# Probabilities split into two float16 parts in SBUF and turned by transposing DMAs, with four PSUM banks for scores

## The chip, the core and the metric

The kernel runs on one core of a Trainium2 chip. The metric is device time in microseconds (us) of one launch. The engines of the core are TensorE (PE; its weight loads are listed apart as PEld), VectorE (DVE), ScalarE (ACT), GpSimd (POOL) and SyncE (SP), which here issues all DMAs from one queue, in order. PE writes to PSUM, which has eight banks of 512 float32 per partition; everything else lies in SBUF.

## What is computed

One layer of a hybrid encoder for 1,024 positions of width 1,024: a layer norm, one input projection into sixteen column groups, four mixers, gates, one output projection, and a second layer norm. Three of the mixers are attentions with four heads of 64, and they are where the change lies:

```python
# B: each chunk of 64 positions sees itself and the 8 chunks before it
s = einsum(q, k) * 64 ** -0.5 + rel_bias;  p = softmax(s);  o = einsum(p, v)
# C: an indexer scores all keys, the best 256 are kept
score = einsum(relu(iq . ik) * 64 ** -0.5, iw * 8 ** -0.5)
_, idx = top_k(score, 256);  p = softmax(q . k[idx] * 64 ** -0.5 + t5_bias);  o = p . v[idx]
# M: 256 memory tokens
p = softmax(q . km * 64 ** -0.5);  o = p . vm
# together (A is a gated MLP over blocks of 128 positions)
mixed = concat(ya * silu(a_g), yb * silu(b_g), yc * silu(c_g), ym * silu(m_g))
out = layer_norm(2 ** 0.25 * h + mixed @ w_out + b_out)
```

## The kernel before

Rows are worked on in eight blocks of 128 (`rb`), heads in pairs (`pair`, `odd`). Float32 operands of projections and scores are split into a high and a low float32r part, and a product is three matmuls (high x high, high x low, low x high). A projection (`project`) is 24 matmuls of 128x512 into one bank; its weight block comes by DMA (`raw`), is rounded by ACT and gets its low part from POOL (`wblk`, line 203).

An attention is a list of items, one per row block and head pair: 16 for memory (M), 16 for band attention (B), 16 for sparse attention (C). Each item has four sorts of parts. `scores` makes the score matmuls into banks `qk`, adds the bias with a running maximum (DVE) and takes the exponential (ACT) into a float32 row tile `sc`, up to 1,024 wide. `turn` transposes up to four 128x128 blocks of `sc` on PE into a bank `pt`; `spread` rounds that to float16 (`ph`, on ACT) and takes the rest (`pl`, on DVE). `values` multiplies both by the values, kept as three bfloat16 parts (`pv_mm`), and normalises. `close` turns the output once on PE, multiplies it by the gate and stores it to `mix_dram`. There are 64, 120 and 144 blocks to turn in M, B and C, 328 in all, in 112 groups.

`parts_of` writes the order: with the scores of an item come the turns and all but the last values of the item before it, the last values of the one before that, and the close of a third. `weave` puts steps of a projection between these parts; a `Filler` step may stand on PE no earlier than the part that lies `LAG` (for output projections `LAG_O`) parts back. `OUT_PER` is how many steps of the output projection follow a part in the last attentions, `OUT_FROM` where that begins. The search for the 256 best scores runs beside it on DVE and ACT (`jka`, `jk`). The final order on each engine is made by the scheduler, which takes these priorities and its own simulated times.

`BANKS` shares out PSUM: 2 banks for projections (`pp`), 2 for scores (`qk`), 3 for transposes (`pt`), 1 for values (`pv`).

Of the kernel before, what the change touches and what calls it, by code (L numbers as in the profile page):

```python
# [11 lines left out]
F32 = mybir.dt.float32  # L12
# [32 lines left out]
LAG_O = 14  # L45
# [9 lines left out]
LAG, LAG_S = 22, 6  # L55
# [20 lines left out]
def tile_trunk(ctx, tc, x, mem, ln_in_g, ln_in_b, w_in, b_in, a_ln_g, a_ln_b, a_ws, a_bs,  # L76
# [112 lines left out]
    def wblock(w, c0, m=P):  # L189
# [4 lines left out]
        if m < P:  # L194
            both = gp.tile([P, 2, 2, KT // 2, m], F32R, tag="planes", bufs=1, name="wnar")
        for q in range(2):
            t = E.tile([P, 2, 4, P], F32R, tag="w", bufs=WB, name="wblk") if m == P else both[:, q]
# [96 lines left out]
    def x_parts(half, xts):  # L294

        high, rest = hT[half]
        for k in range(KT):
            pt = bank(("pt", "qk")[k % 2], "xT")
# [11 lines left out]
    def mem_parts(r, mt):  # L310
        for q in range(2):
            pt = bank("pt")
# [206 lines left out]
    def spread(pt, n):  # L519

        ph = gp.tile([P, 512], F16, tag="ph", bufs=3, name="ph")
        pl = gp.tile([P, 512], F16, tag="pl", bufs=3, name="pl")
# [4 lines left out]
    def pv_mm(pv, j, ph, pl, c, v3, first, last):  # L527
        PE.matmul(pv[:, j * 192:j * 192 + 192], ph[:, c:c + P], v3.rearrange("p t d -> p (t d)"),
                  start=first, stop=False)
        PE.matmul(pv[:, j * 192:j * 192 + 128], pl[:, c:c + P], v3[:, 0:2].rearrange("p t d -> p (t d)"),  # L530
# [18 lines left out]
    gates = {}  # L549

    def gate_of(kt, rb):
        if (kt, rb // 4) not in gates:
            t = gp.tile([P, 512], F32, tag="gate", bufs=2, name="gate")
            SP.dma_start(out=t, in_=gate_dram[kt][rb // 4])
            gates[kt, rb // 4] = t
        c = (rb % 4) * P
        return gates[kt, rb // 4][:, c:c + P]
# [4 lines left out]
    class Item:  # L562
# [3 lines left out]
        def __init__(self, scores, turn, values, close=None):  # L566
            self.scores, self.turn, self.values, self.close = scores, turn, values, close

    def parts_of(items):
# [3 lines left out]
        for t in range(n + 3):  # L573
            now, prev, prev2, prev3 = [items[t - d] if 0 <= t - d < n else None for d in range(4)]
# [56 lines left out]
    def mix_of_m(pair, rb, q):  # L631
# [14 lines left out]

        def turn():
            pt = bank("pt")
            for j in range(4):
                PE.transpose(pt[:, j * P:(j + 1) * P], d["sc"][:, j * P:(j + 1) * P], ident)  # L650
            d["p"] = spread(pt, 512)

        def values():
            ph, pl = d["p"]
            pv = bank("pv")
            for odd in range(2):
                for r in range(2):
                    pv_mm(pv, odd, ph, pl, (2 * odd + r) * P, v3m[pair][:, r, odd], r == 0, r == 1)
            d["o"] = normalized(pv, d["rsum"], 6)

        def close():
            t = small([P, P], "mix")
# [3 lines left out]
        return Item(scores, [turn], [values], close)  # L666

    def mix_of(kt, rb, kb0, st, near, far_of, last):
# [31 lines left out]

        def turn(odd, c):
            sc = d["sc"][odd]
            m = min(4, nk - c)
            pt = bank("pt")
            for j in range(m):
# [610 lines left out]
```

## Time and profile before

| | |
|---|---|
| median of 3 timed runs | 700.78 us (699.7 to 700.86) |
| the profiled execution | 701.02 us, of which the span from first to last instruction is 699.1 |
| PE, DVE, ACT, POOL busy | 660.8, 527.4, 415.7, 259.1 us |
| granted clock of PE, mean | 0.993 |
| DMA | 63.49 MB, all issued by SP |

Busy time is the union of an engine's instructions. Matmuls overlap and their ends are modelled, so the mean duration of a matmul is longer than the slot it takes in the queue; the slot is the distance between starts. A wait is put down to the instruction whose signal came last.

### The profile page before, as it was taken

What the parts mean: (1) busy time and instruction counts of PE and PEld (TensorE: products, weight loads), DVE (VectorE), ACT (ScalarE), POOL (GpSimd) and SP (SyncE); (2) the same over time, 40 slices, a digit from 0 to 9 for tenths busy, and PEclk for the clock granted to TensorE, in tenths of its full rate; (3) what the DMA queues carried; (4) which work ended last, traced back from release to release, by engine and by line L of the source; (5) the groups of instructions that cost most, each with busy time, mean ns of one, the idle gap of its engine ahead of it and who ended that gap; (6) DMA issues with size and microseconds to landing.
All of it is one profiled execution on the core that took longest, in us unless ns stands there. A gap on an engine that the chain in (4) does not pass through costs nothing. (4 is left out here: it accounts for less than half of the span.)

```text
span 699.1 us, 11217 instructions
## 1 busy us (share of the span) xinstructions
PE 660.8 (95%) x3882; PEld 507.6 (73%) x3882; DVE 527.4 (75%) x1376; ACT 415.7 (59%) x865; POOL 259.1 (37%) x254
## 2 busy tenths in 40 slices
PE   4889999999999998989999999999899998999895
PEld 3767877776777776767777777777678676777685
DVE  6684235556868989897787879999965789698735
ACT  4764345554789697967787789465355554344210
POOL 4672212530624554132110221022222536457752
PEclk9999999999999999999999999999999999999998
DMA  9792510311321232222110312122102473134111
GB/s 271 229 340 77 167 31 7 115 46 32 101 82 48 76 107 61 75 84 54 57 39 11 89 33 58 29 65 84 53 5 72 150 253 102 68 118 166 57 61 60
DMA packets 67444, 63.49 MB, mean 91 GB/s; under 512 B 9232, under 2 KB 55612, under 8 KB 67388
## 3 DMA queue, kind: packets, MB, share of 16 engines
q1 hardware_dynamic: 67388, 62.78, 29.4%
q8 instruction: 30, 0.49, 0.3%
q14 instruction: 26, 0.21, 0.1%
HBM read 46.70 MB, written 17.64 MB: 92 GB/s over the span
## 5 line engine op out<-in xcount | busy, mean ns | idle before, releaser
L91 PE MATMUL acc<-hTh,wblk 128*128 128x512 f32 (+1 forms) x960 | 311.1, 395 | 3.2 <-ACT hTh L91 1.3
L91 PEld LDWEIGHTS acc<-hTh,wblk 128*128 128x128 f32 x960 | 176.8, 188 | 48.4 <-issue 10.5
L91 PE MATMUL acc<-hTl,wblk 128*128 128x512 f32 (+1 forms) x480 | 186.5, 389 | 0.0
L203 POOL TENSOR_TENSOR wblk<-raw,wblk 128x512 fp32r<-128x512 f32 x72 | 99.1, 1380 | 191.0 <-ACT wblk L91 186.5
L91 PEld LDWEIGHTS acc<-hTl,wblk 128*128 128x128 f32 x480 | 90.4, 188 | 17.5 <-issue 1.8
L91 ACT ACTIVATE jka<-score,cand 128x768 int8<-128x768 f32 (+2 forms) x93 | 96.6, 1039 | 8.3 <-DVE cand L91 6.1
L91 ACT ACTIVATE ph<-pt 128x512 f16<-128x512 f32 (+3 forms) x112 | 51.4, 476 | 37.7 <-PE pt L91 34.8
L91 DVE TENSOR_TENSOR pl<-pt,ph 128x512 f16<-128x512 f32 (+3 forms) x112 | 59.4, 540 | 12.7 <-ACT ph L91 12.2
L91 ACT ACTIVATE sc<-sc,nb 128x640 f32<-128x640 f32 (+7 forms) x64 | 46.6, 730 | 37.4 <-DVE nb L91 37.2
L91 DVE SCALAR_TENSOR_TENSOR score<-relu,iw,score 128x384 f32<-128x384 f32 (+5 forms) x42 | 45.1, 1078 | 20.0 <-ACT relu L91 17.4
L91 ACT ACTIVATE wblk<-raw 128x512 fp32r<-128x512 f32 x72 | 44.5, 628 | 23.5 <-PE acc L91 13.4
L91 PE MATMUL pt<-ident,sc 128*128 128x128 f32 x328 | 57.2, 280 | 0.0
L91 PE MATMUL acc<-woh,mh 128*128 128x512 f32 (+1 forms) x144 | 55.7, 387 | 0.0
L91 PE MATMUL acc<-wol,mh 128*128 128x512 f32 (+1 forms) x144 | 54.2, 377 | 0.0
L91 PE MATMUL acc<-woh,ml 128*128 128x512 f32 (+1 forms) x144 | 54.0, 377 | 0.0
L91 ACT ACTIVATE relu<-sc 128x384 f32<-128x384 f32 (+2 forms) x80 | 36.3, 530 | 25.9 <-PE sc L91 25.8
L91 PE MATMUL pv<-v,ph 128*128 128x192 bf16 x264 | 47.0, 249 | 3.2 <-ACT ph L91 2.6
L91 PEld LDWEIGHTS <-ph 128*128 128x128 f16 x328 | 32.1, 98 | 18.9 <-issue 9.9
L91 PEld LDWEIGHTS pt<-ident,sc 128*128 128x128 f32 x328 | 38.5, 142 | 7.3 <-issue 1.9
L91 PE MATMUL pv<-v,pl 128*128 128x128 bf16 x264 | 43.7, 222 | 0.1
L91 PEld LDWEIGHTS <-pl 128*128 128x128 f16 x328 | 31.6, 98 | 12.3 <-DVE pl L91 3.5
L91 DVE TENSOR_SCALAR_CACHE_REDUCE jk<-planes,lo 128x384 bf16<-128x384 uint16 (+2 forms) x48 | 35.7, 744 | 1.0
(206 smaller groups left out, 1255.9 us busy)
## 6 DMA issues: line engine op xcount, KB each, us to landing
raw<-in_w_in SPq DMA_DIRECT2D x32, 512.0 KB, 3.9
xt<-in_x SPq DMA_DIRECT2D x8, 512.0 KB, 8.6
h_dram<-xt SPq DMA_DIRECT2D x8, 512.0 KB, 5.8
gate<-t SPq DMA_DIRECT2D x16, 256.0 KB, 2.1
rawo<-in_w_out SPq DMA_DIRECT2D x8, 512.0 KB, 4.7
hr<-h_dram SPq DMA_DIRECT2D x8, 512.0 KB, 6.2
out<-hr SPq DMA_DIRECT2D x7, 512.0 KB, 2.7
gate<-gate SPq DMA_DIRECT2D x13, 256.0 KB, 2.7
```

Of the source, the lines that this page charges most:

```text
L91: ins = op(*a, **k)
L203: G.tensor_sub(t[:, 1], r, f32(t[:, 0]))
```

## The change

The two parts of the probabilities are made in SBUF, before they are turned: ACT rounds `sc` to float16, POOL subtracts (`part`). Both parts are written where there is room, mostly in the second half of the `sc` tile seen as float16 (`row`), or over the scores already used. A transposing DMA, issued by SP, then turns up to eight 128x128 blocks into a tile `pT`, of which there are six (`turn`). An item of 512 keys or fewer takes one such DMA for each head (an M item one for both), one of 640 two, one of 768 and more three: 124 in all. PE's 328 transposes of probabilities and `spread` are gone; the turn of the output in `close` stays on PE.

Scores get four banks, transposes one. `parts_of` has no turns any more: all of an item's values come two items after its scores. The gates are loaded in pieces of 128x128, one per item, in place of 128x512. Weight tiles go from five to four, and the lags and shares of the woven projections change.

```diff
-LAG_O = 14
+LAG_O = 9
...
-LAG, LAG_S = 22, 6
+LAG, LAG_S = 15, 4
...
-C1_ORDER, C1_HELD, HELD_PARTS, HELD_STEPS = "k0 k1 v1 q1 v0 g1", "q0 g0", 5, 16
-OUT_FROM, OUT_PER = 3, 1
-S4, EV, WB, SB, BOOST = 8, 4, 5, 4, 400
-BANKS = {"pp": 2, "qk": 2, "pt": 3, "pv": 1}
+C1_ORDER, C1_HELD, HELD_PARTS, HELD_STEPS = "k0 k1 v1 q1 v0 g1", "q0 g0", 2, 16
+OUT_FROM, OUT_PER = 2, 1.5
+S4, EV, WB, SB, BOOST = 8, 4, 4, 4, 400
+TB = 6
+BANKS = {"pp": 2, "qk": 4, "pt": 1, "pv": 1}
...
-                accs = [bank(("qk", "pt")[odd], "sc") for odd in range(2)]
+                accs = [bank("qk", "sc") for _ in range(2)]
...
-    def spread(pt, n):
...
-        S.activation(ph[:, :n], pt[:, :n], AF.Copy)
-        V.tensor_sub(pl[:, :n], pt[:, :n], ph[:, :n])
-        return ph, pl
...
+    def turned(sc, n):
...
+        row, nb = sc.bitcast(F16), n // P
+
+        def part(a, b, high, rest):
+            S.activation(high, sc[:, a:b], AF.Copy)
+            G.tensor_sub(rest, sc[:, a:b], high)
+
+        def turn(t, a, src):
+            SP.dma_start_transpose(out=t[:, a:a + src.shape[-1] // P, :], in_=src)
+
+        t = gp.tile([P, KT, P], F16, tag="pT", bufs=TB, name="pT")
+        if 4 * n <= 2048:
+            part(0, n, row[:, 2 * n:3 * n], row[:, 3 * n:4 * n])
+            turn(t, 0, row[:, 2 * n:4 * n])
+            return [t[:, j] for j in range(nb)], [t[:, nb + j] for j in range(nb)]
+        u = gp.tile([P, KT, P], F16, tag="pT", bufs=TB, name="pT")
+        if 3 * n <= 2048:
+            high = row[:, 2 * n:3 * n]
+            part(0, n, high, row[:, :n])
+            turn(t, 0, high)
+            turn(u, 0, row[:, :n])
+            return [t[:, j] for j in range(nb)], [u[:, j] for j in range(nb)]
+        if 2 * n + 512 <= 2048:
+            high = row[:, 2 * n:2 * n + 512]
+        else:
+            high = gp.tile([P, 512], F16, tag="high", bufs=2, name="high")
+        part(0, 512, high, row[:, :512])
+        turn(t, 0, high)
+        part(512, n, row[:, 512:n], row[:, 1024:512 + n])
+        turn(u, 0, row[:, :n])
+        turn(t, 4, row[:, 1024:512 + n])
+        return ([(t, u)[j > 3][:, j] for j in range(nb)], [(u, t)[j > 3][:, j] for j in range(nb)])
...
+    def gate_of(kt, rb):
+        t = gp.tile([P, P], F32, tag="gate", bufs=2, name="gate")
+        SP.dma_start(out=t, in_=gate_dram[kt][rb // 4][:, (rb % 4) * P:(rb % 4 + 1) * P])
+        return t
...
             if prev2:
-                parts.append(prev2.values[-1])
-            if prev:
-                parts.append(prev.turn[0])
-            if prev3 and prev3.close:
+                parts.append(prev2.values[0])
+            if prev3:
                 parts.append(prev3.close)
-            if prev:
-                for turn, values in zip(prev.turn[1:], prev.values):
-                    parts += [turn, values]
+            if prev2:
+                parts += prev2.values[1:]
...
                 S.activation(sc[:, :n], sc[:, :n], AF.Exp, bias=nb, accum_out=d["rsum"][:, odd:odd + 1])
-
-        def turn(odd, c):
-            sc = d["sc"][odd]
-            m = min(4, nk - c)
-            pt = bank("pt")
-            for j in range(m):
-                PE.transpose(pt[:, j * P:(j + 1) * P], sc[:, (c + j) * P:(c + j + 1) * P], ident)
-            d["p", odd, c] = spread(pt, m * P)
+                d["p", odd] = turned(sc, n)
```

What this moves on PE, at the end of a band item's values in the second pair (before; `ph` and `pl` are the float16 parts, `o` the output of an earlier item, `acc` a projection):

```order
L91 LDWEIGHTS ph_4368
L91 MATMUL pv_4321<-v3_3150,ph_4368 128x192
L91 LDWEIGHTS pl_4369
L91 MATMUL pv_4321<-v3_3150,pl_4369 128x128
L91 MATMUL pt_4464<-ident_66,o_4278 128x128
L91 MATMUL pt_4471<-ident_66,sc_4229 128x128
L91 MATMUL pt_4492<-ident_66,sc_4230 128x128 x4
L91 MATMUL acc_4612<-hTl1_116,wblk_4286 128x512
```

And the same sort of place after, where the values of the item two back follow the scores (`qk`) of a later one:

```order
L92 MATMUL qk_5172<-kl_3933,qh_3664 128x256
L92 MATMUL qk_5173<-kl_3933,qh_3664 128x256
L92 MATMUL acc_5121<-hTh0_113,wblk_5117 128x512
L92 MATMUL acc_5121<-hTl0_114,wblk_5117 128x512
L92 MATMUL acc_5121<-hTh0_113,wblk_5117 128x512 x2
L92 LDWEIGHTS pT_4966
L92 MATMUL pv_5206<-v3_4195,pT_4966 128x192
L92 LDWEIGHTS pT_4967
L92 MATMUL pv_5206<-v3_4195,pT_4967 128x128
```

The transposes of `sc` no longer stand between values and projections; the weights of the value matmuls are slices of `pT`, which DMAs fill.

SP's queue where memory attention begins, after (before, the weight loads stand there without anything between them; `raw` is a weight block, `mix` the output of an item, `gate` a gate):

```order
L193 DMA raw_2620<-in_w_in 128x8x128
L531 DMA_TRANSPOSE pT_2088<-sc_2085 128x8x128
L193 DMA raw_2628<-in_w_in 128x8x128
L531 DMA_TRANSPOSE pT_2131<-sc_2128 128x8x128
L193 DMA raw_2852<-in_w_in 128x8x128
L531 DMA_TRANSPOSE pT_2157<-sc_2154 128x8x128
L531 DMA_TRANSPOSE pT_2218<-sc_2215 128x8x128
L584 DMA mix0_101<-mix_2272 128x128
L580 DMA gate_2440<-gate6_0_97 128x128
L531 DMA_TRANSPOSE pT_2301<-sc_2298 128x8x128
```

The transposing DMAs stand in the one queue behind loads that wait for buffers and behind stores that wait for earlier items' outputs, and those stand behind them.

## Rows read from the trace of the kernel before

**Rows 1.** The page's head: busy us of each engine, share, instructions.
```profile
span 699.1 us, 11217 instructions
PE 660.8 (95%) x3882; PEld 507.6 (73%) x3882; DVE 527.4 (75%) x1376; ACT 415.7 (59%) x865; POOL 259.1 (37%) x254
```

**Rows 2.** Stretches: busy PE, PEld, DVE, ACT, POOL; clock, DMA share, GB/s.
```profile
204.00:333.00 129.00, 121.94 (x723) 93.77 (x723) 113.89 (x336) 106.17 (x233) 51.70 (x68) 1.00 0.26 74
333.00:483.00 150.00, 149.41 (x891) 111.74 (x891) 129.92 (x446) 109.47 (x233) 26.24 (x21) 1.00 0.18 52
483.00:545.00 62.00, 59.62 (x380) 45.82 (x379) 47.55 (x125) 29.07 (x60) 16.34 (x16) 1.00 0.19 58
545.00:655.00 110.00, 105.33 (x663) 80.09 (x661) 90.81 (x236) 50.94 (x117) 65.66 (x59) 0.98 0.40 131
655.00:699.10 44.10, 36.45 (x201) 31.61 (x200) 22.95 (x39) 4.98 (x10) 19.31 (x20) 0.93 0.16 62
```

**Rows 3.** The chain that ended last, from 655 us: start, us, what.
```profile
662.65 28.81 PE acc L91 x172
...
691.49 0.43 DVE hr L91
...
695.32 0.66 DVEq L1312
```

**Rows 4.** The page's groups of turns and splits: busy us, mean ns, idle.
```profile
L91 ACT ACTIVATE ph<-pt 128x512 f16<-128x512 f32 (+3 forms) x112 | 51.4, 476 | 37.7 <-PE pt L91 34.8
L91 DVE TENSOR_TENSOR pl<-pt,ph 128x512 f16<-128x512 f32 (+3 forms) x112 | 59.4, 540 | 12.7 <-ACT ph L91 12.2
...
L91 PE MATMUL pt<-ident,sc 128*128 128x128 f32 x328 | 57.2, 280 | 0.0
```

**Rows 5.** PE's timeline in the late attentions: start us, us, instruction.
```profile
601.71 0.60 PE L91 MATMUL pt<-ident,sc 128*128 128x128 f32 x4
602.07 0.48 PE L91 MATMUL acc<-woh,mh 128*128 128x512 f32 x1
602.38 0.40 PE L91 MATMUL acc<-wol,mh 128*128 128x512 f32 x1
602.62 0.39 PE L91 MATMUL acc<-woh,ml 128*128 128x512 f32 x1
```

**Rows 6.** Groups by form on ACT and POOL.
```profile
L91 ACT ACTIVATE wblk<-raw 128x512 fp32r<-128x512 f32 x72 | 44.5, 628 | 23.5 <-PE acc L91 13.4 <-DMA raw<-in_w_in 4.7 <-DMA raw<-in_w_mem_kv 3.2
L91 ACT ACTIVATE ph<-pt 128x512 f16<-128x512 f32 x60 | 35.1, 590 | 23.8 <-PE pt L91 23.7
L91 ACT ACTIVATE sc<-sc,nb 128x640 f32<-128x640 f32 x20 | 16.4, 824 | 5.3 <-DVE nb L91 5.3
...
L203 POOL TENSOR_TENSOR wblk<-raw,wblk 128x512 fp32r<-128x512 f32 x72 | 99.1, 1380 | 191.0 <-ACT wblk L91 186.5 <-PE sc L91 1.9 <-PE qk L91 1.8
L1176 POOL TENSOR_TENSOR hr<-hr,bo 128x1024 f32<-128x1024 f32 x7 | 17.7, 2543 | 0.1
```

**Rows 7.** Waits of PEld and SP: who for whom, us in total, times, longest.
```profile
PEld L91 <- ACT ph L91: 5.5, 4, 2.8
PEld L91 <- DVE pl L91: 3.5, 5, 1.8
PEld qk L91 <- DVE mx L91: 2.9, 4, 2.1
PEld acc L91 <- POOL wblk L203: 2.2, 2, 1.1
...
SPq L192 <- POOL wblk L203: 157.7, 28, 25.2
```

**Rows 8.** DMA issues: KB each, median us from issue to landing.
```profile
raw<-in_w_in SPq DMA_DIRECT2D x32, 512.0 KB, 3.9
...
gate<-gate SPq DMA_DIRECT2D x13, 256.0 KB, 2.7
...
bias<-in_b_in SPq DMA_DIRECT2D x1, 13.0 KB, 8.0
```

**Rows 9.** The tile `sc`: ns min/median/max, first and last start us, forms.
```profile
L91 ACT ACTIVATE sc<-sc,nb x64: 386/768/1152, 335.3 to 639.0; 128x640 f32<-128x640 f32 x20, 128x128 f32<-128x128 f32 x8, 128x256 f32<-128x256 f32 x8, 128x384 f32<-128x384 f32 x8
...
L91 ACT ACTIVATE sc<-qk,nb x32: 463/474/491, 204.3 to 326.8; 128x256 f32<-128x256 f32 x32
...
L91 DVE CUSTOM_DVE_ANT_0 sc<-qk,farB x24: 285/552/558, 346.6 to 469.9; 128x384 f32<-128x384 f32 x16, 128x128 f32<-128x128 f32 x4, 128x256 f32<-128x256 f32 x4
L91 DVE CUSTOM_DVE_ANT_0 sc<-qk,nearB,mx x24: 472/480/485, 347.1 to 476.3; 128x256 f32<-128x256 f32 x24
```

More of the change, by code (lines that the diff above doesn't have):

```diff
@@ L194, in wblock @@
         if m < P:
-            both = gp.tile([P, 2, 2, KT // 2, m], F32R, tag="planes", bufs=1, name="wnar")
+            narrow = [gp.tile([P, 2, KT // 2, m], F32R, tag=tag, bufs=1, name="wnar") for tag in ("planes", "score6")]
         for q in range(2):
-            t = E.tile([P, 2, 4, P], F32R, tag="w", bufs=WB, name="wblk") if m == P else both[:, q]
+            t = E.tile([P, 2, 4, P], F32R, tag="w", bufs=WB, name="wblk") if m == P else narrow[q]
             r = raw[:, 4 * q:4 * q + 4, :m]
@@ L297, in x_parts @@
         for k in range(KT):
-            pt = bank(("pt", "qk")[k % 2], "xT")
+            pt = bank("qk", "xT")
             for j in range(4):
@@ L311, in mem_parts @@
         for q in range(2):
-            pt = bank("pt")
+            pt = bank("qk", "mT")
             for j in range(4):
@@ L516, in tile_trunk, with pv_mm @@
                 V.memset(score[rb][0:64, (rb + 1) * P - 64:(rb + 1) * P], LOW)
[L519 to L528 removed]
+    def turned(sc, n):
[27 more added lines that the diff above has]
+        return ([(t, u)[j > 3][:, j] for j in range(nb)], [(u, t)[j > 3][:, j] for j in range(nb)])
+    def pv_mm(pv, j, ph, pl, v3, first, last):
+        PE.matmul(pv[:, j * 192:j * 192 + 192], ph, v3.rearrange("p t d -> p (t d)"),
                   start=first, stop=False)
[L530 removed]
+        PE.matmul(pv[:, j * 192:j * 192 + 128], pl, v3[:, 0:2].rearrange("p t d -> p (t d)"),
                   start=False, stop=last)
@@ L562, in tile_trunk, with __init__ @@
     class Item:
-        def __init__(self, scores, turn, values, close=None):
-            self.scores, self.turn, self.values, self.close = scores, turn, values, close
+        def __init__(self, scores, values, close):
+            self.scores, self.values, self.close = scores, values, close
     def parts_of(items):
@@ L573, in parts_of @@
         for t in range(n + 3):
-            now, prev, prev2, prev3 = [items[t - d] if 0 <= t - d < n else None for d in range(4)]
+            now, _, prev2, prev3 = [items[t - d] if 0 <= t - d < n else None for d in range(4)]
             if now:
@@ L645, in scores @@
                              bias=nb[:, odd:odd + 1], scale=0.125, accum_out=d["rsum"][:, odd:odd + 1])
[L647 to L651, printed above, removed]
+            d["p"] = turned(d["sc"], 512)
         def values():
@@ L657, in values @@
                 for r in range(2):
-                    pv_mm(pv, odd, ph, pl, (2 * odd + r) * P, v3m[pair][:, r, odd], r == 0, r == 1)
+                    pv_mm(pv, odd, ph[2 * odd + r], pl[2 * odd + r], v3m[pair][:, r, odd], r == 0, r == 1)
             d["o"] = normalized(pv, d["rsum"], 6)
         def close():
-            t = small([P, P], "mix")
+            t = small([P, P], "mix", 2)
             gated(d["o"], gate_of(6 + pair, rb), t)
             store_mix(6 + pair, rb, t)
-        return Item(scores, [turn], [values], close)
+        return Item(scores, [values], close)
     def mix_of(kt, rb, kb0, st, near, far_of, last):
@@ L721, in mix_of @@
         steps = [(odd, c) for odd in range(2) for c in chunks]
-        return [Item(scores, [lambda s=s: turn(*s) for s in steps], [lambda s=s: values(*s) for s in steps], close)]
+        return [Item(scores, [lambda s=s: values(*s) for s in steps], close)]
     def queries_of_m(pair, q):
@@ L1046, in last @@
             def last(write, rb=rb):
-                t = small([P, P], "mix")
+                t = small([P, P], "mix", 2)
                 write(t)
@@ L1096, in last @@
             else:
-                t = small([P, P], "mix")
+                t = small([P, P], "mix", 2)
                 write(t)
@@ L1104, in tile_trunk @@
     weave(parts_of([it for rb in C0_FIRST for it in mixes_of_c0(rb)]), C[1].all(C1_ORDER), C1_STEPS)
-    gates.pop((4, 0), None)
     L = None
@@ L1121, in load @@
                 low = L.tile([P, KT, P], F32R, tag="ml", bufs=MHB, name="ml")
-                raw = L.tile([P, KT, P], F32, tag="mixt", bufs=2, name="mixt")
-                lows, raws = [[t[:, 0:4, :], t[:, 4:8, :]] for t in (low, raw)]
+                lows = [low[:, 0:4, :], low[:, 4:8, :]]
+                raws = [L.tile([P, 4, P], F32, tag="mixt", bufs=2, name="mixt") for _ in range(2)]
             else:
@@ L1140, in column @@
         def column(k, write):
-            t = small([P, P], "mix")
+            t = small([P, P], "mix", 2)
             write(t)
```

12 lines of the change are left out of this document (2 added, 10 removed).

## The prediction

> **What bounds the kernel now.** I read the page's head first: in a span of 699.1 us TensorE (PE) is busy for 660.8 and VectorE (DVE) for 527.4 [rows 1]. The profiled execution took 701.02 us, 1.9 more than its span; the three timed runs have a median of 700.78, so the sum below is made against 701.0 and stands for the median too. Those shares are averages, so I cut the span at the attention stages: memory attention 204 to 333 us, band attention 333 to 483, the first sparse attentions 483 to 545, the late ones 545 to 655, and the rest of the output projection [rows 2]. In the four attention stages PE is busy 121.9 of 129, 149.4 of 150, 59.6 of 62 and 105.3 of 110 us. DVE is the nearest rival: 113.9 of 129 and 129.9 of 150 in the first two. ScalarE (ACT) has 106.2 of 129, GpSimd (POOL) at most 65.7 of 110. The last stage is one chain: 172 output matmuls in a row for 28.8 us, then about 7 us of normalising and storing [rows 3]. So what the change takes off PE comes off the time, as long as nothing new holds PE up.
>
> **What is taken off PE.** 328 transposes of 128x128 blocks go; each is a row of its own group, 57.2 us busy in all, mean 280 ns [rows 4]. That mean is a latency: matmuls overlap. The timeline shows the slot. Four transposes start at 601.71, the next matmul at 602.07; that one's follower comes 0.31 us later, where two undisturbed 512-column matmuls start 0.24 apart [rows 5]. Four transposes so hold PE for 0.36 + 0.07 = 0.43 us, 0.1075 each: 328 x 0.1075 = **35.3 us**. The lower end is the bare slot (0.36 / 4 = 0.09, 29.5 us), the upper the busy share (57.2 us). I take 35.3, since the starts are what PE's queue is made of.
>
> [...]
>
> **What is taken off ACT and DVE.** The 112 rounding copies out of PSUM (51.4 us on ACT) and the 112 differences (59.4 us on DVE) go [rows 4]. ACT gets the copies back at SBUF: a 512-column copy there is 0.63 us against 0.59 out of PSUM [rows 6], so ACT stays as it is. DVE keeps the gain, 59.4 us of its 527; it is not the engine that ends the stages, so I book nothing, but it lowers the nearest rival. The waits of PE's weight loads for these parts go too: 5.5 us for the high and 3.5 for the low ones [rows 7], together **9.0 us**.
>
> **What POOL gets.** The differences move to it: 328 blocks of 128 columns at 1,380 ns per 512 [rows 6], 0.345 us a block, 113 us. Memory and band attention have 64 + 120 blocks, 63 us beside the 51.7 + 26.2 that POOL does there in 279 us [rows 2]: room. The C stages have 144 blocks, 50 us. The late order holds 96 of them (all of the second pair's 72, and 24), 33 us beside 65.7 in 110 us: 99, nearly full (a rival below).
>
> **What SP gets.** 124 transposing DMAs for 656 blocks (328 high, 328 low), 21.5 MB, and gates loaded in 48 pieces of 64 KB where 13 loads of 256 KB stand now. The trace has no transposing DMA. From below: a plain load of 256 KB, as much as the largest of these, lands in 2.7 us [rows 8]. From above: if it moved in small pieces, the biases are the nearest row, 13 KB as 3,328 elements of 4 bytes, 8.0 us [rows 8]; 32-byte pieces would be 8,192 for 256 KB, 2.5 times as many, 20 us. I take 3 to 5 us, because the source is read in rows of 256 bytes or more, and the loads of weights in 512-byte rows land 512 KB in 3.9 us [rows 8].
>
> [...]
>
> **Is that hidden?** An item's probabilities are now used two items after its scores. The 64 exponentials of band and sparse attention, two to an item, start from 335.3 to 639.0 [rows 9]: 9.5 us per item; memory attention's 32 start from 204.3 to 326.8: 7.7 us. So some 15 to 19 us lie between. The changed order bears it out: priced at 0.24 us per 512-column matmul [rows 5], the work between an item's last score matmul and its first value matmul is mostly 13 to 21 us, and about 6 us for two items early in memory attention. Against it stands, for 640 keys: four reductions of about 0.5 us [rows 9], an exponential and a copy at 0.82 and about 0.79 (0.63 scaled by 640 / 512), two differences of 1.72 on POOL (1.38 scaled alike) [rows 6]: about 2 + 1.6 + 3.4 = 7, with queues 8. So up to about 8 us of DMA is hidden. Behind the waiting transposes in SP's queue stand weight and gate loads; behind values on PE stands everything else. For the two short items, the fill of each stage, and transposes held in SP's queue I book new waits, from nothing to 20 us, and take **9 us**, as much as the old waits.
>
> **Edits booked at nothing.** Four score banks in place of two: PE's weight loads waited 2.9 us in all on the reductions that free them [rows 7]; a gain of at most that. One bank for the gate transposes: one small transpose per item, 9.5 us apart. Four weight tiles in place of five: PE waits 2.2 us for POOL's weight parts now [rows 7]; the next block's preparation, 2 x 0.63 on ACT and 2 x 1.38 on POOL, is covered by the 48 matmuls of a block's two halves, 48 x 0.24 = 11.5 us. Without that cover a block costs its 4 us. The other lags only move projection work among the attentions: PE's amount stays, and the last 172 matmuls and 7 us stay.
>
> **The sum.** 701.0 - 35.3 - 9.0 + 9 = 665.7, **666 us** (5% less). About 0.2%, 1.4 us, is what a measurement of this kernel can tell from no change.
>
> **Rivals.**
> - *POOL ends the late attentions (or SP holds the transposes).* For: 99 of 110 us worked out above, in a stage that would itself shrink by 96 x 0.1075 = 10; additions of 2.54 us for 1,024 columns stand in POOL's queue ahead of differences [rows 6]. And SP's queue already stands still 157.7 us for POOL's weight parts in 28 waits, one of 25.2 [rows 7]; a transpose behind such a load is late. Against: the output rows' additions can slide into the last stage, where POOL has 19.3 of 44 us. It gives back the late stage's 10 us and some 10 of queueing: 675 to 698, about 685. Chance 0.25.
> - *The transposes are slow* (the other side). One mechanism: small pieces. It decides from a landing time of about 9 us on: 48 items, each later by landing less 8, cost 48 us for each us, against a gain of 35.3 + 9 = 44. At 11 us: 48 x 3 = 144, 701 - 44 + 144 = 801. For: the bias row. Against: reads in long rows, 18 to 40% busy DMA engines [rows 2]. Chance 0.14.
> - *PE gets back the busy share*, 57.2 us, with no new waits: 701 - 57.2 - 9 = 635; 634 to 644. For: DVE is lighter, banks are freer. Chance 0.09.
> - *Each transpose is worth its full latency*, 328 x 0.28 = 92 us: 701 - 92 = 609. Against: starts 0.09 us apart [rows 5]. Chance 0.01. [...]
> - *The transposes go but the new waits eat all 44 us*: no change. Chance 0.03.
>
> **How the numbers follow.** The forecast case, 644 to 674, has 0.48: 0.48 + 0.25 + 0.14 + 0.09 + 0.01 + 0.03 = 1. Faster by over 0.2% is 0.48 + 0.25 + 0.09 + 0.01 = 0.83, within 0.2% 0.03, slower 0.14. The range leaves out the slow case, the even one and the 609: 634 to 698, 0.82 inside.
>
> **What would show each step.** PE's busy time falls by about 57 us to some 604 and 328 transposes are gone; a group of transposes in the late timeline no longer stands between output matmuls. DVE falls to about 468, POOL rises to about 372 with the differences at some 1.4 us per 512 columns. The DMA transposes land 3 to 5 us after issue, and PE's waits for DMA stay under about 10 us. Wrong would be: landing times above 9 us; waits of PE for DMA of tens of us; POOL without idle time from the first late attention on; or a DVE that was the real limit in band attention, which would show as a stage shortened by more than 120 x 0.1075 = 13 us.

## The result: one per cent slower

The changed kernel took 707.8 us (median of 4 runs, 705.2 to 708.6), the kernel before on the same chip 700.8 us: ratio 1.0096, 95% interval 1.0068 to 1.0124. The forecast was 666 us, the range 634 to 698, so the time lies on the other side. The profiled execution took 708.57 us, 1.8 more than its span. The head of its page, for [rows 1]:

```profile
span 706.8 us, 11033 instructions
PE 640.8 (91%) x3554; PEld 484.4 (69%) x3554; DVE 494.7 (70%) x1264; ACT 414.9 (59%) x845; POOL 355.6 (50%) x346
```

The 328 transposes are gone from PE, yet its busy time fell by 20 us and not by 57, and its idle time (span less busy time) rose from 38.3 to 66.0 us. The same kind of stretches as in [rows 2], cut at the changed kernel's own milestones (last index score, first band score, first masked sparse score, last value matmul, end; columns as in [rows 2]):

```profile
203.30:343.30 140.00, 124.94 (x707) 97.83 (x707) 112.19 (x318) 108.56 (x234) 72.44 (x86) 0.95 0.44 104
343.30:507.70 164.40, 156.51 (x920) 117.67 (x920) 145.86 (x468) 124.53 (x257) 70.71 (x61) 0.98 0.51 107
507.70:664.00 156.30, 136.65 (x766) 99.73 (x765) 103.31 (x276) 71.34 (x152) 115.43 (x108) 0.93 0.68 156
664.00:706.80 42.80, 34.63 (x198) 30.37 (x197) 23.24 (x38) 6.14 (x11) 24.42 (x25) 0.94 0.26 96
```

Cut at the same milestones, the kernel before has its last index score at 186.1 us and then stages of 146.2, 170.1, 153.6 and 43.1 us. So the index stage (all up to the last index score), which holds no transposed probabilities at all, ends **17.2 us later**; memory attention gives back 6.2 us, band attention with the search 5.7, and the sparse stage is 2.7 longer. PE now stands idle for 15, 8 and 20 us of the three attention stages, where it was 7, 3 and 5, and its mean granted clock is 0.95, 0.98 and 0.93 where it was 1.00, 1.00 and 0.98.

**The index stage.** PE's timeline (start us, us, instruction) at one of the last pairs of index heads, before the change: each row holds both heads (x2, one start).

```profile
184.43 0.50 PE L91 MATMUL sc<-ikh,iqh 64*128 64x512 f32 x2
184.76 0.40 PE L91 MATMUL sc<-ikh,iql 64*128 64x512 f32 x2
185.00 0.40 PE L91 MATMUL sc<-ikl,iqh 64*128 64x512 f32 x2
```

A like place after: the even head starts alone, two projection matmuls follow, then the odd head, one matmul behind the even one (its first stands with the even head's second, both at 177.84).

```profile
176.75 0.50 PE L92 MATMUL sc<-ikh,iqh 64*128 64x512 f32 x1
177.18 0.72 PE L92 MATMUL acc<-hTh,wblk 128*128 128x512 f32 x2
177.84 0.50 PE L92 MATMUL sc<-ikh,iqh 64*128 64x512 f32 x1
177.84 0.73 PE L92 MATMUL sc<-ikh,iql 64*128 64x512 f32 x2
178.18 0.62 PE L92 MATMUL sc<-ikl,iqh 64*128 64x512 f32 x2
```

Before, three such steps start within 0.80 us (184.43 to the next pair at 185.23). After, the same six matmuls take 0.43 (176.75 to 177.18) and 0.88 (177.84 to the next projection at 178.72). In the order of instructions all 120 steps stood side by side before; now 20 are split. In the trace the two heads of a step start together, within 0.03 us, in 36 of 120 steps instead of all 120. Taken from start to start, between the first and the last index score, the index matmuls take 36.0 us instead of 29.0, and the projection matmuls among them 90.7 instead of 79.8 (391 of them instead of 348). In the x2 rows before, the two heads of a pair run side by side: 0.24 us from 184.76 to 185.00 for two heads of 512 columns, as long as one matmul of 512 columns takes [rows 5].

**The way by DMA.** The tile `pT` in the changed kernel (ns min/median/max of the issues on SP's queue, who waited for the tile in us and times, then the landing):

```profile
L531 SPq DMA_TRANSPOSE pT<-sc x116: 1167/1217/3532, 222.6 to 658.9; - x116
L531 SPq DMA_TRANSPOSE pT<-high x8: 1194/1213/1269, 517.8 to 573.3; - x8
...
  PEld L92: 19.7, 18
  DVE sc L92: 17.2, 8
  PE pv L92: 13.7, 9
...
DMA to landing us min/median/max: 2.3/3.1/8.7
```

The landing is as forecast. The waits of PE (13.7 us) and of its weight loads (PEld, 19.7) overlap: counted once they are 19.8 us. The waits for `pT` given below are sums of both, 33.3 us here. What the forecast never priced stands in the first row: each transposing DMA holds SP's queue 1.22 us, where a plain one of the same bytes takes 0.47 (measured below): 124 x 1.22 = 151 us by the median, and the issues add up to 161, of one queue that also issues every load and store. SP's timeline in the late stage:

```profile
565.68 1.19 SPq L531 DMA_TRANSPOSE pT<-high  x1
567.06 2.76 SPq L531 DMA_TRANSPOSE pT<-sc  x2
569.92 1.09 SPq L332 DMA_DIRECT2D gate<-t  x1
571.31 1.29 SPq L531 DMA_TRANSPOSE pT<-sc  x1
572.70 0.54 SPq L1248 DMA_DIRECT2D rawo<-in_w_out  x1
```

And PE's timeline at the same place: a wait of 3.63 us for a transposed tile (in brackets), and output matmuls whose starts lie 0.57 and 0.43 us apart behind it, 0.22 to 0.23 ahead of it. The mean granted clock is 1.00 from 560 to 568 us and 0.50 from 572 to 577.

```profile
567.92 0.39 PE L92 MATMUL acc<-wol,mh 128*128 128x512 f32 x1
568.14 0.39 PE L92 MATMUL acc<-woh,ml 128*128 128x512 f32 x1
572.16 2.32 PE L92 MATMUL pv<-v,pT 128*128 128x128 bf16 x16 [3.63 <-DMA pT<-sc]
...
575.87 0.78 PE L92 MATMUL acc<-woh,mh 128*128 128x512 f32 x1
576.44 0.63 PE L92 MATMUL acc<-wol,mh 128*128 128x512 f32 x1
576.87 0.63 PE L92 MATMUL acc<-woh,ml 128*128 128x512 f32 x1
```

From 560 to 610 us the mean granted clock is 0.86, and the DMA engines are busy for 0.96 of the stretch. In the kernel before (second row) the same 50 us have 0.97 and 0.43. Columns as in [rows 2]:

```profile
560.00:610.00 50.00, 39.88 (x228) 28.25 (x227) 30.02 (x79) 26.04 (x53) 37.91 (x38) 0.86 0.96 206
560.00:610.00 50.00, 47.95 (x315) 36.56 (x313) 42.75 (x113) 22.85 (x52) 24.79 (x23) 0.97 0.43 145
```

### The profile page after: what moved, and what is told of

It reads as the page before. It is cut to its first block, busy times and chain, and to the rows that moved or that the text cites. A ratio compares the mean times of both kernels' runs of the same rounds, so it can differ in the third digit from the quotient of the medians.

```text
span 706.8 us, 11033 instructions
## 1 busy us (share of the span) xinstructions
PE 640.8 (91%) x3554; PEld 484.4 (69%) x3554; DVE 494.7 (70%) x1264; ACT 414.9 (59%) x845; POOL 355.6 (50%) x346
## 4 chain that ended last, share of the span: by engine, by line
PE 40%; DVE 21%; DMA 10%; issue 10%; ACT 8%; POOL 6%; SPq 3%; DVEq 0%; POOLq 0%; ACTq 0%
PE acc L92 30%; DMA pT<-sc 6%; DVE jk L92 5%; PE sc L92 5%; ACT jka L92 3%; DVE sc L92 3%; PE pv L92 3%; DVE o L92 2%; POOL sc L528 2%; PE qk L92 2%; DMA raw<-in_w_in 2%; ACT sc L92 2%; DVE planes L92 1%; DMA mixt<-mix 1%; DVE vt L92 1%
## 5 line engine op out<-in xcount | busy, mean ns | idle before, releaser
L92 PE MATMUL acc<-hTh,wblk 128*128 128x512 f32 (+1 forms) x960 | 317.7, 399 | 8.1 <-ACT t L92 3.4
L92 PEld LDWEIGHTS acc<-hTh,wblk 128*128 128x128 f32 x960 | 179.5, 190 | 57.0 <-issue 9.0
L528 POOL TENSOR_TENSOR sc<-sc 128x512 f16<-128x512 f32 (+4 forms) x84 | 92.0, 1109 | 56.4 <-ACT sc L92 24.8
L92 ACT ACTIVATE jka<-score,cand 128x768 int8<-128x768 f32 (+2 forms) x93 | 96.5, 1037 | 15.8 <-DVE cand L92 12.9
L92 PEld LDWEIGHTS <-pT 128*128 128x128 f16 x656 | 49.0, 103 | 44.5 <-issue 22.7
L92 PE MATMUL pv<-v,pT 128*128 128x192 bf16 (+1 forms) x528 | 55.4, 241 | 16.9 <-DMA pT<-sc 13.7
L92 ACT ACTIVATE wblk<-raw 128x512 fp32r<-128x512 f32 x72 | 44.8, 626 | 32.6 <-PE acc L92 17.6
L92 DVE SCALAR_TENSOR_TENSOR score<-relu,iw,score 128x384 f32<-128x384 f32 (+5 forms) x42 | 45.6, 1095 | 19.6 <-ACT relu L92 17.2
L92 ACT ACTIVATE sc<-sc 128x512 f16<-128x512 f32 (+4 forms) x84 | 45.6, 570 | 4.5 <-POOL sc L528 4.0
L92 DVE TENSOR_REDUCE o<-pv 128x128 f32<-128x384 f32 x48 | 26.2, 545 | 13.5 <-PE pv L92 13.5
L92 DVE TENSOR_SCALAR_CACHE_REDUCE jk<-planes,cand 128x384 bf16<-128x384 bf16 (+2 forms) x45 | 33.4, 742 | 1.1
L92 DVE SCALAR_TENSOR_TENSOR t<-t,xh 128x512 f32<-128x512 f32 x24 | 23.7, 987 | 12.9 <-ACT t L92 12.2
L92 PE MATMUL qk<-kh,qh 64*128 64x384 f32 (+3 forms) x96 | 27.9, 419 | 5.2 <-DVE mx L92 5.2
```

What stands on the lines that cost most here:

```text
L92: ins = op(*a, **k)
L528: G.tensor_sub(rest, sc[:, a:b], high)
```

## The experiments

Theories at the start: **A**, the index heads lost their separate bank tags and so their pairing; **B**, POOL's queue delays the differences in the late stage; **C**, the transposing DMAs themselves are the loss; **D**, VectorE and ScalarE, with the search on them, end the stages once PE is lighter; **E**, the new lags and paces. Ratios are to the kernel before on the same chip.

### Which part of the change, first round

**Banks by head.** The four score banks as two tags of two.

```
-BANKS = {"pp": 2, "qk": 4, "pt": 1, "pv": 1}
+BANKS = {"pp": 2, "qk": 2, "qo": 2, "pt": 1, "pv": 1}
-accs = [bank("qk", "sc") for _ in range(2)]
+accs = [bank(("qk", "qo")[odd], "sc") for odd in range(2)]      # attention scores and xT alike
```

> The changed kernel with its four score banks as two tags of two, so that the two heads of a pair never take banks out of one rotation (index heads, memory, band and sparse scores). Theory A (the shared rotation lets the odd head's matmul come later than the even one's, and that costs the 17 us by which the last index score ends late): the last index score matmul goes back from 203.3 us to 186 to 192, its group's busy time from 68 to about 46 to 52, and the time from 708 to 691 to 698. Rival (the loss sits in the late sparse attentions, with GpSimd or the DMAs, and the front is slack that the search fills): last index score as in A or not, but the time stays 704 to 709. If pairs have nothing to do with it, the last index score stays at 200 to 205.

Measured: 706.3 us (1.0077, 1.0051 to 1.0102); the last index score at 204.6 us, 48 of 120 steps start together. Theory A as it was put is wrong: the shared rotation is not the cause.

**The kernel before with fewer banks for the index heads.**

```
-accs = [bank(("qk", "pt")[odd], "sc") for odd in range(2)]
+accs = [bank("pt", "sc") for odd in range(2)]
```

> The kernel before with one edit: both index heads of a pair take their banks from the three-bank tag (in place of one from the two-bank and one from the three-bank tag). Theory A: index stage gets longer as in the changed kernel, last index score from 186 to 196 to 206, time from 700.8 to 705 to 715. Rival (the index stage's length comes from something else, such as four weight tiles or the order of the projections): last index score within 3 us of 186, time within 2 us of 700.8.

Measured: 716.7 us (1.0222, 1.0175 to 1.0269), the last index score at 215.3, 3 of 120 steps start together. With three banks it is later than with four; before there were five, two for even heads and three for odd. That leads to the new theory **A2**: the number of banks decides. A spare bank for the odd head would let a pair start as soon as the even head's is free; without it the odd head waits for its own, and a projection is put between.

**Differences on VectorE.**

```
-G.tensor_sub(rest, sc[:, a:b], high)
+V.tensor_sub(rest, sc[:, a:b], high)
```

> The changed kernel with the differences (rest of the float16 parts) on VectorE instead of GpSimd in every item. Theory B (in the late sparse attentions the differences stand behind weight parts, row differences and additions in GpSimd's queue, so the transposes start late): GpSimd's busy time falls by 92 us to about 264, TensorE's waits for transposed tiles fall from 33 us to under 15, the time falls by 5 to 15 us to 693 to 703. Rival C (the transposing DMAs themselves are late): waits stay at 25 us or more, time within 3 us of 708. Rival D (VectorE, with the search in it, ends the band stage): the band stage gets longer by up to 20 us, time 708 to 725.

Measured: 719.2 us (1.0260, 1.0211 to 1.0309). The waits for `pT` fall to 24 us, not under 15, and the search ends at 524.0 us instead of 514.4: VectorE has no such time to give. Rival D's line held.

**Plain copies for transposing DMAs** (the probabilities are not turned).

```
-SP.dma_start_transpose(out=t[:, a:a + src.shape[-1] // P, :], in_=src)
+SP.dma_start(out=t[:, a:a + src.shape[-1] // P, :], in_=src.rearrange("p (j c) -> p j c", c=P))
```

> The changed kernel with plain DMA copies of the same blocks in place of the transposing DMAs (the probabilities are then not turned; sizes, places and order are the same). Theory C (DMA cost of the transposes: 1.2 us of SP each, landing 3 to 9 us, DMA engines 0.96 busy in part of the late stage): issue falls to about 0.35 us, landing to 2 to 2.5 us, TensorE's waits for transposed tiles from 33 us to under 12, time falls by 8 to 15 us to 693 to 700. Theory B or A (GpSimd's queue, or the split pairs in front): waits fall by a third at most, time 704 to 709.

Measured: 697.9 us (0.9953, 0.9929 to 0.9976); issue 0.47 us, landing 2.3 us, the waits for `pT` 15.6 instead of 33.3 us. C holds some 10 us.

```profile
L531 SPq DMA_DIRECT2D pT<-sc x116: 464/471/1691, 223.5 to 648.5; - x116
DMA to landing us min/median/max: 1.8/2.3/6.9
```

### The fifth bank

**Five banks.** Even heads from a tag of two, odd heads from a tag of three, which the gated outputs' transposes share.

```
-BANKS = {"pp": 2, "qk": 4, "pt": 1, "pv": 1}
+BANKS = {"pp": 2, "qk": 2, "qo": 3, "pv": 1}
```

> The changed kernel with five banks open to the index scores again: the even head's from a tag of two, the odd head's from a tag of three, which the transposes of the gated outputs share (so no bank for them alone). Theory A2 (the fifth bank, not the shared rotation, is what let both heads of a pair start together, and what kept 35 more projection matmuls from being placed ahead of the last index score): all 120 pairs start together again, the last index score ends at 185 to 190 instead of 203.3, the search ends 10 to 15 us earlier, and the time falls from 708 to 690 to 698, below the kernel before by 0.4 to 1.5%. Rival (the front's loss is work moved ahead, so it is paid back later): last index score at 185 to 190, time 703 to 708.

Measured: the last index score at 186.6 us, all 120 steps start together; 702.05 us (1.0004, 0.9980 to 1.0027), between the two lines and 1 us from the rival's. A2 holds for the stage, but only 5.8 of its 17 us reach the end. Its stages (as above):

```profile
186.60:331.00 144.40, 130.26 (x725) 101.34 (x724) 122.58 (x345) 115.17 (x248) 76.76 (x88) 0.95 0.44 108
331.00:493.80 162.80, 149.37 (x859) 114.04 (x859) 146.53 (x439) 118.44 (x245) 69.25 (x60) 0.96 0.50 101
493.80:653.60 159.80, 138.51 (x819) 103.43 (x819) 105.54 (x278) 72.58 (x154) 116.12 (x107) 0.97 0.65 159
653.60:697.60 44.00, 36.30 (x205) 31.62 (x204) 22.75 (x36) 6.14 (x11) 26.28 (x27) 0.97 0.25 93
```

The sparse stage is 6.2 us longer than before although PE has 144 transposes less in it. PE is busy 626.2 us and idle 71.4. This kernel is the base of what follows.

**The kernel before with four banks.**

```
-BANKS = {"pp": 2, "qk": 2, "pt": 3, "pv": 1}
+BANKS = {"pp": 2, "qk": 2, "pt": 2, "pv": 1}
```

> The kernel before with its three-bank tag cut to two, one bank of PSUM left unused: the index scores have four banks as in the changed kernel, and nothing else of the change is made. Theory A2: the last index score moves from 186 to 200 to 205, about a third of the pairs no longer start together, and the time rises by 8 to 17 us to 709 to 718. Rival (the front's loss comes from another part of the change, as four weight tiles): last index score at 184 to 190, time 700 to 705.

Measured: 721.4 us (1.0259, 1.0210 to 1.0308), the last index score at 207.2, 39 steps start together. The stage answers as A2 says. The time is above its line, 709 to 718, and here nearly all of the stage's 21 us reaches the end: the stages behind it add up to 513.5 us, 513.0 before. The turned probabilities lost a bank too; what that costs was not measured apart.

**Lags and pace of the kernel before** in the changed kernel.

```
-LAG_O = 9
+LAG_O = 14
-LAG, LAG_S = 15, 4
+LAG, LAG_S = 22, 6
-OUT_FROM, OUT_PER = 2, 1.5
+OUT_FROM, OUT_PER = 3, 1
```

> The changed kernel with the lags and the pace of the output projection of the kernel before (22, 6 and 14; from item 3, one part each). Theory E (these settings, chosen for the new order, cost or give something by themselves): time moves by more than 3 us either way. Theory A2 and C (banks and DMAs hold the loss): last index score stays at 203, time 705 to 712.

Measured: 720.8 us (1.0283, 1.0239 to 1.0328). The time moves by more than the 3 us of E's line, but upwards: the settings are no part of the loss; without them it is 13 us more.

### What holds the five-bank kernel

Theories from here on: **C2**, what is left is the low part's way, above all its DMAs; **B2**, its differences on GpSimd; **D** as above.

**Five banks and plain copies:** the two diffs above together.

> The same five banks, and plain DMA copies in place of the transposing DMAs (probabilities not turned). Theory A2 plus C (two separate losses that add): the 10 us that plain copies saved on the changed kernel come on top of those of the five banks: 680 to 688. Rival (both act on the same waits, those of the search and of the late stage): 688 to 697, little better than five banks alone or copies alone.

Measured: 695.6 us (0.9921, 0.9884 to 0.9958): the rival's line; 6.5 us less than five banks, 2.3 less than copies alone. The two losses do not add.

**Half of the search left out,** in both kernels.

```
-for b in range(15, -1, -1):
+for b in range(15, 15):
```

Before:

> The kernel before with the second half of the search's bits left out (16 of 31 counting steps on VectorE and ScalarE; the low 16 bits of the thresholds are then not found). Taken for the difference to the same cut in the five-bank kernel. If TensorE alone bounds the kernel before (theory of the prediction), the time falls by little, to 694 to 700. If the search also holds it, to 670 to 690.

Measured: 697.9 us (0.9950, 0.9929 to 0.9971), 3.3 us less, the line of TensorE alone. Five banks:

> The changed kernel with five banks for the index scores and the same half of the search left out. Theory D (with the transposes gone from TensorE, the search and the attentions' work on VectorE and ScalarE set the end of the band stage, so TensorE's gain there turns into idle time): the time falls by 15 us or more, to 670 to 687, and by at least 10 us more than the same cut takes off the kernel before. Rival C2 (the late stage with its transposing DMAs holds the loss): the cut takes about as much off both kernels, within 5 us.

Measured: 690.6 us (0.9864, 0.9832 to 0.9897), 11.5 us less (9.8 by the ratios). The search takes 6 to 8 us more from the changed kernel, less than D said and more than C2 said: D has a share, smaller than it said.

**GpSimd relieved in the late stage.**

```
-ML_V = (6,)
+ML_V = (0, 1, 2, 3, 4, 5, 6, 7)
-(V if k % 2 < half * WO_V else G).tensor_sub(lo[:, c], raw[:, c], f32(hi[:, c]))
+V.tensor_sub(lo[:, c], raw[:, c], f32(hi[:, c]))
```

> Five banks for the index scores, and in the late stage GpSimd's low parts of the mixed rows and of the output weights are made on VectorE. Theory B (the differences wait in GpSimd's queue in the late stage, which has no gap there): GpSimd's busy time in the late 100 us falls from 84 to about 60, TensorE's waits for transposed tiles there fall from 23 us to under 12, the time to 690 to 697. Rivals C2 and D: the waits stay at 18 us or more, time 699 to 708.

Measured: 701.2 us (0.9998, 0.9969 to 1.0028), POOL busy 336 instead of 360 us (from 545 to 645 us, 67.7 instead of 80.1: a smaller relief than expected), the waits for `pT` 34.5 us, with five banks 28.9. B's line failed; the run without differences, below, settles it.

**Only the high part,** made and turned (the low part is left out; its matmuls use the high part).

```
-G.tensor_sub(rest, sc[:, a:b], high)
-u = gp.tile([P, KT, P], F16, tag="pT", bufs=TB, name="pT")
-turn(u, 0, row[:, :n])                    # and the low blocks of the other cases
```

> Five banks for the index scores, and only the high float16 part is made and turned (the low part's matmuls use the high part again, so TensorE has the same work; the low part of the probabilities is left out of the result): no differences on GpSimd, half of the transposed bytes, at most one transposed tile for each head. Theory C2 (what is left of the loss is the way of the probabilities through GpSimd and the transposing DMAs): the late sparse stage falls from 160 to 138 to 145 us, the time to 672 to 685. Rival D (memory and band attention are held by VectorE and ScalarE with the search in them, the late stage by its other work): the time only reaches the 695 that plain copies gave, 690 to 698.

Measured: 675.9 us (0.9646, 0.9618 to 0.9675): 26.1 us less, most of it in the sparse stage, 144.5 us:

```profile
186.70:323.90 137.20, 128.20 (x725) 101.05 (x724) 113.62 (x329) 112.08 (x242) 59.44 (x73) 0.95 0.38 98
323.90:483.00 159.10, 151.38 (x881) 114.78 (x881) 136.86 (x453) 120.94 (x251) 30.17 (x23) 0.97 0.35 80
483.00:627.50 144.50, 133.13 (x784) 99.77 (x783) 96.55 (x276) 71.96 (x154) 75.29 (x68) 0.95 0.57 142
```

So the low part's way is the largest loss. It has three pieces, taken apart next.

**Differences made, low part not turned.**

```
-u = gp.tile([P, KT, P], F16, tag="pT", bufs=TB, name="pT")
-turn(u, 0, row[:, :n])
-return [t[:, j] for j in range(nb)], [u[:, j] for j in range(nb)]
+return [t[:, j] for j in range(nb)], [t[:, j] for j in range(nb)]
```

> Five banks, the differences on GpSimd are made, but the low part is not turned: no DMA for it and no second tile (its matmuls use the high part again, so the low part is left out of the result). If DMAs or tiles carry the 26 us (theory C2): 674 to 684. If GpSimd's differences carry it (theory B2): 694 to 702.

Measured: 683.2 us (0.9737, 0.9697 to 0.9778), 18.8 us less than five banks, with 92 transposing DMAs in place of 124 and half of their bytes. The 7.3 us (6.4 by the ratios) by which it stays above the run before are the differences, which are still made here.

**No differences, every DMA and tile kept** (the high part is turned twice; up to 512 keys ScalarE makes a second copy of it).

```
-G.tensor_sub(rest, sc[:, a:b], high)
-turn(u, 0, row[:, :n])
+turn(u, 0, high)
```

> Five banks, no differences on GpSimd; every transposing DMA and tile is there, in size and number, but turns the high part twice (the low part is left out; up to 512 keys, ScalarE makes the second copy). Theory B2: 674 to 684. Theory C2: 694 to 702. If both have a share: 684 to 694.

Measured: 701.9 us (0.9993, 0.9967 to 1.0019): nothing.

```profile
PE 629.6 (90%) x3554; PEld 481.7 (69%) x3554; DVE 487.7 (70%) x1264; ACT 431.8 (62%) x893; POOL 261.2 (37%) x254
```

The span is 700.8 us, so PE is idle for 71.2, as with five banks. The DMAs carry the loss with or without the differences on GpSimd. Two things blur this: ScalarE has 18.5 us more to do, and more of the output projection comes last (240 output matmuls behind the last value matmul instead of 203), so that the sparse stage is 10.5 us shorter and the last one 15.8 longer.

**Only the high part, three tiles:** `TB = 6` becomes `TB = 3`.

> Only the high part, as in the run that took 676 us, but with three transposed tiles in place of six, so that, as with both parts and six tiles, one and a half of the large items fit. If the number of tiles carries the loss (DMAs and VectorE wait for a tile until the matmuls of an earlier item have used it): 685 to 700. If not: 674 to 680.

Measured: 674.9 us (0.9626, 0.9583 to 0.9669), as with six tiles. The tiles are no part of it.

**Copies in halves:** each plain copy is issued as two of 64 partitions.

```
-SP.dma_start(out=t[:, a:a + src.shape[-1] // P, :], in_=src.rearrange("p (j c) -> p j c", c=P))
+for p in (0, 64):
+    SP.dma_start(out=t[p:p + 64, a:a + src.shape[-1] // P, :], in_=src[p:p + 64].rearrange("p (j c) -> p j c", c=P))
```

> Five banks and plain copies in place of the transposing DMAs (probabilities not turned), each issued as two copies of 64 partitions: 248 issues instead of 124, the same bytes and the same packets. If the issuing queue's time carries the loss: its time for these goes from 58 to some 115 us (transposes: 151), and the time from 695.6 with whole copies to 699 to 703, as with transposes. If the DMA engines' time carries it: 693 to 698, as with whole copies.

Measured: 708.4 us (1.0085, 1.0054 to 1.0115), 12.8 us more than with whole copies (11.5 by the ratios), and more than with transposing DMAs, above both lines. 248 issues of 0.58 us (median) are 145 us of the queue; landing is 2.2 us, as with whole copies. The heads of the pages, whole copies first:

```profile
span 696.2 us, 11061 instructions
PE 632.4 (91%) x3554; PEld 488.0 (70%) x3554; DVE 499.3 (72%) x1264; ACT 413.3 (59%) x845; POOL 361.0 (52%) x346
span 706.6 us, 11377 instructions
PE 633.6 (90%) x3554; PEld 484.2 (69%) x3554; DVE 497.5 (70%) x1264; ACT 413.5 (59%) x845; POOL 366.0 (52%) x346
```

PE is idle for 63.8 us with whole copies, 73.0 with halves and 71.4 with transposes. So a queue that is held about as long as by the transposes is enough to bring PE's idle time back. The rest, that PE is busy 7 us longer than with transposes, has no cause shown. Not quite apart is the time of the DMA engines: their share in the whole span rose from 39.0 to 43.4%, in the sparse stage from 0.51 to 0.60, but stays under the 47.9% and 0.65 of the five-bank kernel, which is faster.

### A version that keeps what pays

**Sparse attentions as before the change** (turned by TensorE, old order, lags and output pace), memory and band attention by DMA, five banks.

```
-return mix_of(4 + pair, rb, 0, C[pair].stacks(), near, lambda lo, hi: score[rb][:, lo:hi], last)
+return mix_of_c(4 + pair, rb, 0, C[pair].stacks(), near, lambda lo, hi: score[rb][:, lo:hi], last)
```

Here `mix_of_c` is the function of the kernel before, which turns by TensorE.

> Five banks; memory and band attention turn their probabilities by DMA as in the changed kernel, the sparse attentions by TensorE in the order, with the lags and the output pace of the kernel before. If the changed order pays in memory and band attention and costs in the sparse stage (there the five-bank kernel is 6 us longer than the kernel before, though 144 transposes are gone): 690 to 696, faster than both kernels. If what memory and band attention gain is only handed on to the search: 699 to 705.

Measured: 700.2 us (0.9969, 0.9945 to 0.9993), the second line. The first masked sparse score comes 10 us earlier than before (491.9 us), but the sparse stage is 10 us longer: 408 projection and output matmuls of 512 columns lie in it instead of 366. Projections that filled PE in band attention are left over for later, while PE idles 13 of 161 us there.

**Only the eleven late ones as before;** the first five sparse attentions are turned by DMA as well.

```
-return mix_of_c(4 + pair, rb, 0, C[pair].stacks(), near, lambda lo, hi: score[rb][:, lo:hi], last)
+return (mix_of if not pair and rb in C0_FIRST else mix_of_c)(4 + pair, rb, 0, C[pair].stacks(), near, lambda lo, hi: score[rb][:, lo:hi], last)
```

> Five banks; transposes by DMA in memory and band attention and in the first five sparse attentions, by TensorE in the order of the kernel before in the eleven late ones. If the changed order pays wherever the DMA engines are not full: TensorE has 48 transposes, about 5 us, less than in the hybrid with all sparse attentions on TensorE, and the time is 693 to 698. If TensorE is not what the first sparse attentions wait for: 698 to 704.

Measured: **695.6 us** (0.9903, 0.9874 to 0.9932), faster than both kernels. The head of its page:

```profile
span 691.7 us, 11120 instructions
PE 633.3 (92%) x3650; PEld 486.5 (70%) x3650; DVE 513.3 (74%) x1296; ACT 412.9 (60%) x849; POOL 332.1 (48%) x318
```

And its stages, columns as above:

```profile
186.80:330.50 143.70, 128.91 (x724) 100.10 (x724) 121.88 (x345) 115.20 (x248) 77.99 (x88) 0.96 0.44 109
330.50:493.10 162.60, 148.20 (x854) 112.92 (x854) 144.97 (x439) 118.47 (x245) 69.17 (x60) 0.96 0.50 102
493.10:649.70 156.60, 149.85 (x928) 112.16 (x928) 115.65 (x310) 73.04 (x159) 96.02 (x87) 1.00 0.44 128
649.70:691.70 42.00, 34.40 (x198) 30.21 (x196) 20.94 (x37) 4.98 (x10) 17.05 (x18) 0.96 0.20 74
```

PE is busy 149.9 of 156.6 us in the sparse stage at clock 1.00, against 138.5 of 159.8 at 0.97 with five banks and DMAs throughout. SP's waits between 550 and 600 us, summed, are 42.2 us here, 37.6 in the kernel before (552 to 602), 17.6 with five banks and 11.6 with copies in halves: a queue that waits is one that has time to issue. This does not order all kernels: it is 22.1 in the changed kernel, which is slower than five banks, and 25.5 with the high part alone, which takes 20 us less than this one.

## Why the prediction was wrong

**The step that failed first: "Four score banks in place of two".** That holds for the attentions. The index heads had five banks, two for even heads and three for odd, and now have four. The order of instructions, which was there to read, has 20 split pairs in place of none. The term was booked as a gain of at most 2.9 us; it cost 17.2 us in its stage and 5.8 at the end (five banks: 707.8 to 702.05).

**The step that failed most: "Is that hidden?"** One item's way was set against the 15 to 19 us between scores and values, and the landing of 3 to 5 us was right (3.1). What was not counted is what the queue pays: 1.22 us for each of 124 issues, in order, with every other load. The new waits, taken as 9 us so that they cancel the old ones, were mis-sized: PE and its weight loads waited 19.8 us for `pT`, counted once, and VectorE 17.2 us for score tiles that DMAs still read. With five banks PE's busy time falls by 34.6 us, where the sum had 35.3 (partly luck, since the mean granted clock is 0.969 and not 0.993), and its idle time rises by 33.1, where the sum had nothing. Leaving the low part's DMAs out gives 18.8 us, its whole way 26.1. The rival that named SP put the delay on GpSimd, behind weight loads; relieving GpSimd gave nothing.

**"What the change takes off PE comes off the time"** held only while PE had nothing else to wait for. With the low part's way gone and five banks the kernel takes 675.9 us, 10 above the 665.7 of the sum; the search, half of which takes 6 to 8 us more from the five-bank kernel than from the one before, could be most of that, but it was not cut in this kernel. The three parts, 5.8 + 26.1 + 10.2, are the 42.1 us by which the forecast missed. The first two were measured one on top of the other, so each stands for its place in that row, not for itself; the third is what is left.

**Right** were the mechanism, that TensorE's transposes are worth taking off (675.9 us with the high part's DMAs alone, and 695.6 in a complete kernel), the landing time, and four weight tiles at nothing: PE's weight loads wait 2.4 us for POOL's weight parts, 2.2 before [rows 7]. POOL was put at 372 us and has 356, DVE at 468 and has 495, PE at 604 and has 641, the index stage's unpaired matmuls and slower clock among it (626 with five banks). Of DVE's 27 us GpSimd's differences are the larger part: the same 1,264 VectorE instructions take 507.0 us with five banks and 487.7 without the differences, 497.1 and 483.0 when the low part is not turned. The slot of 0.1075 us for a transpose [rows 5] was not measured apart.

**Open:** why copies of both parts (695.6) stay 12 us above turning the high part alone (683.2), though they hold the queue for less time (58 us by the medians, 110 with the 92 transposes). With copies SP stands 85.6 us for GpSimd's differences, in order, and nothing behind them is issued; that this is the reason was not tried. How much of the loss is the queue's time and how much that of the DMA engines, 0.96 busy in part of the late stage, is not settled either: leaving DMAs out takes away both. Loads and stores issued by another engine, with the transposes left on SP, would have been the direct trial and were not run. Nor was a second queue for the transposes.

## What to carry to other kernels

Price a DMA by the time that it holds the queue that issues it, times its number (here 1.22 us, 124 times), beside its landing (3.1 us): a queue is an engine with a busy time of its own. When tags of buffers are merged, count for each user how many it had and has, and read in the order of instructions whether work that ran side by side still stands side by side. And move work off the bounding engine only where the way round has room: here up to the first sparse attentions, not in the late ones, where loads and stores use the same queue and the DMA engines were 0.96 busy.

## What the runs showed of the hardware

A product of two SBUF operands on VectorE waited for the GpSimd instruction that ran beside it. The operation `o<-o,ri` (128x128, 32 times) has a mean of 471 ns before, with POOL busy 259 us, and 618 in the changed kernel, with POOL 356 us:

```profile
L92 DVE TENSOR_TENSOR o<-o,ri 128x128 f32<-128x128 f32 x32 | 19.8, 618 | 0.5
```

With the differences on VectorE, POOL 264 us:

```profile
L92 DVE TENSOR_TENSOR o<-o,ri 128x128 f32<-128x128 f32 x32 | 14.7, 458 | 0.1
```

POOL's total does not set the mean: it is 557 ns with the high part alone, POOL 262 us, and 722 with all sparse attentions as before, POOL 318 us. What stands beside each one does. In nine kernels 117 of these operations have no GpSimd instruction beside them: they take 260 to 295 ns. In seven kernels, the one before among them, 68 take over 600 ns, and each ends 0.13 to 0.16 us after a GpSimd instruction ends. Not each meeting costs that much: some with a GpSimd instruction beside them take under 300 ns. One of the long ones, from the kernel before (583.43 + 2.38 = 585.81, 583.68 + 2.29 = 585.97):

```profile
583.43 2.38 POOL L1176 TENSOR_TENSOR hr<-hr,bo 128x1024 f32<-128x1024 f32 x1
583.68 2.29 DVE L91 TENSOR_TENSOR o<-o,ri 128x128 f32<-128x128 f32 x1
```

Some 5 of the 27 us by which DVE missed its forecast are this one operation.
